# A GLA recurrence on one Trainium2 core: where the output projection's weight sums are held and how many transfers they take, and when the operands of its later products are split

## The chip, the cores and the metric

The kernel runs on one core of a Trainium2 chip. The metric is the time of one execution in device microseconds (us), the median of three executions of the same program. The engines are named as in the profile: PE (TensorE matmul), PEld (its weight loads), DVE (VectorE), ACT (ScalarE), POOL (GpSimd) and SP, whose queue issues the DMA transfers of this kernel.

## The reference

A trunk of two layers over 1024 tokens of width 1024, in float32. Each layer is a token mixer followed by a SwiGLU feed-forward block, both behind an RMS norm and modulated by a conditioning vector `c`. Layer 0 mixes with softmax attention with a forget gate, layer 1 with gated linear attention (GLA). The change lies in layer 1's mixer:

```python
def gated_linear_attention(h, w_in, w_a2, b_a, g_o, w_out):
    q, k, v, r, a_lr = jnp.split(h @ w_in, [512, 1024, 2048, 3072], axis=-1)
    log_alpha = jax.nn.log_sigmoid(a_lr @ w_a2 + b_a) / 16.0
    # 4 heads, 16 chunks of 64 tokens; key width 128, value width 256
    b = jnp.cumsum(log_alpha, axis=2)
    q_in, k_in = q * jnp.exp(b), k * jnp.exp(-b)
    A = jnp.where(tril, jnp.einsum('bnthk,bnshk->bnhts', q_in, k_in), 0.0)
    o_intra = jnp.einsum('bnhts,bnshv->bnthv', A, v)
    kv = jnp.einsum('bnshk,bnshv->bnhkv', k * jnp.exp(b_last[:, :, None] - b), v)
    def step(state, xs):                       # state: (heads, 128, 256)
        dec, kv_n = xs
        return dec[..., None] * state + kv_n, state
    _, s_prev = lax.scan(step, state0, (jnp.exp(b_last), kv))
    o = o_intra + jnp.einsum('bnthk,nbhkv->bnthv', q_in, s_prev)
    o = o * lax.rsqrt(jnp.mean(o * o, axis=-1, keepdims=True) + EPS)   # per head
    return (o.reshape(B, S, 1024) * g_o * jax.nn.silu(r)) @ w_out
```

`x = x + g1 * gla(h)` then goes into the last feed-forward block, and a final RMS norm ends the trunk.

## The kernel before

**Number format.** Every float32 operand of a matmul is held as two parts, hi (a rounding of the value, made by an ACT cast) and lo (the rest, made by a subtraction on DVE or POOL). A product is three matmuls, hi by lo, lo by hi and hi by hi (lines 305, 306 and 307 of the helper `mm3`). `split` (lines 174 and 175) makes the two parts, so each split is one ACT and one DVE instruction. Engines execute their instructions in program order: whatever waits holds up all that stands behind it on its engine or in its queue.

**Stages.** Layer 0 is done by about 1250 us. Then comes layer 1's norm, its first value and gate projections, and from about 1300 to 1640 us the recurrence, one head after the other:

- `head_front` projects keys and queries (tiles `gk_b`, `gqp_b`), scales them with the gate's exponentials and splits them (`gq..`).
- `head_back` computes, in two groups `g` of 512 tokens, the chunks' inner products (`at_b`, masked into `atz_s`, split into `ahl_s`), the outputs `go_b` from the values `gvt_s` and from the state, the state `Sf` (L2115) and its split `S_t`. Each pair of chunks is normalised into `on_t` (L2163; POOL's power for it is L2161), transposed (`ogt_b`, L2125) and multiplied into the gated tile `gs_s` (L2128). The projection of the gate `r` (`gr_b`) is woven between these steps by a planner's costs.
- At a head's end its two `gs_s` tiles (128x1024) go to DRAM (`og_d`, L2280) for heads 0 to 2; those of head 3 stay.
- `gate_body` then makes the next head's exponentials on ACT, and `gv_body` projects its values (`gv_b`, split into `gvt_s`) from two weight tiles `wv_0` and `wv_4`.

**Weights.** Every projection weight is loaded into a ring `wr` of three slots (L227) and split from there by ACT and POOL, the last quarter by DVE (L246). A load into a slot waits until that slot's last reader is done, and so do all transfers behind it in the SP queue. The `ada` work (`ad_s`, loads L442, sums on DVE L505) computes modulation vectors for later stages in the gaps; its loads stand in the same SP queue, its sums in the same DVE program.

**Output projection.** `o @ w_out` is done on blocks of 2x2 with seven products in place of eight, in four column groups `g`. It needs sums of blocks of `w_out`: `ow_sums(h)`, called once a head from `head_front`, loads the four blocks of group `h` into two ring slots (`pw_s`, L971), runs four POOL instructions (L974 to L980) and stores four sums (`ow`, L983). `ow` (L990, L1004, L1005) loads and splits them again later. On the side of `o` the sums are made in `early_t` (heads 0 and 1, woven into head 3) and `out_blocks` (the rest). The products, in the order of the weight index: B11 (`ow` tiles 0 to 3), T2 (4 to 7) and T3 (8 to 11) accumulate in the PSUM banks `oc`; T1 (12 to 15) and B22 (16 to 19) in `oe`; B21 and T4 follow in `out_ends`. `out_add` (L2302) adds a finished bank into the tiles `x`: `x_0`, `x_2`, `x_4` and `x_6` are added first from the B11 product, then from T2. The T3 product of group 0 goes on in the bank that T2's `x_0` addition reads, and so on for the other groups.

**Order.** A scheduler orders the instructions of each engine by priority and due times. `behind_all` makes instructions stand behind those that the table `split_after` names, which before is the last T3 split (L2326). `ob_split(name, j, ...)` makes the split operand of product `name` for the block `j` (tiles `goB` and `goT`).

## Time and profile before

| | |
|---|---|
| median of three executions | 2371.12 us (2369.95 to 2371.66) |
| profiled execution, its own time | 2371.09 us |
| its span, first to last instruction | 2369.4 us |
| granted TensorE clock, mean | 0.998 |
| busy: PE, PEld, DVE, ACT, POOL | 2343.2, 1993.9, 1787.3, 1121.9, 1104.7 us |
| data moved | 375.00 MB, 158 GB/s over the span |

The profile is of one execution: 1.7 us of its time lie outside the span. A row of a timeline reads: start, duration, engine, line, operation, output<-inputs, tile size, count, and in brackets the idle time before it with what ended it. A tile's name has lost its number there. Rows of waits read: engine, line and tile that waited, what it waited for, then total us, times, longest us. "SPq" is SP's queue: a row with it says what a DMA's issue waited for.

### The profile page before, as it was taken

To read this page: it belongs to the slowest core of one execution; us is meant where nothing else is said; L and a number is where in the kernel's file an instruction comes from. 1 tells how busy PE (TensorE), PEld (TensorE's weight loads), DVE (VectorE), ACT (ScalarE), POOL (GpSimd) and SP (SyncE) were. 2 spreads that over 40 slices of the span, in tenths; PEclk is the share of its full clock that TensorE was granted. 3 is DMA by queue.
4 is the path that set the end of the run, shared out by engine and by line. 5 is a ranking of instruction groups with operands and counts; after the bars stand their busy time and mean duration, and the time that the engine had idled before them with its cause. 6 is when DMAs were issued, how large, how long until landed. Compare 5 with 4: busy or idle time off the path is not lost.

```text
span 2369.4 us, 35786 instructions
## 1 busy us (share of the span) xinstructions
PE 2343.2 (99%) x12208; PEld 1993.9 (84%) x12208; DVE 1787.3 (75%) x2994; ACT 1121.9 (47%) x2186; POOL 1104.7 (47%) x995
## 2 busy tenths in 40 slices
PE   8999999999999999999999999999999999999999
PEld 7888888888888888888888899887888888888888
DVE  6577787886688888876788665668787777875787
ACT  6556566665443333345325644344444333345326
POOL 1334444533445665653363432245356665643262
PEclk9999999999999999999999999999999999999999
DMA  8423333332435555457665453454434544457664
GB/s 259 148 77 114 105 121 94 121 126 98 142 103 168 187 165 168 163 195 256 227 210 165 132 148 110 118 185 161 138 106 163 178 147 151 147 200 257 226 201 150
DMA packets 349998, 375.00 MB, mean 158 GB/s; under 512 B 25756, under 2 KB 287032, under 8 KB 349816
## 3 DMA queue, kind: packets, MB, share of 16 engines
q1 hardware_dynamic: 349816, 372.72, 47.9%
q8 instruction: 96, 1.57, 0.3%
q14 instruction: 86, 0.70, 0.1%
HBM read 275.56 MB, written 97.06 MB: 157 GB/s over the span
## 4 chain that ended last, share of the span: by engine, by line
PE 83%; DVE 7%; DMA 3%; issue 2%; POOL 2%; ACT 2%; SPq 1%; DVEq 0%; POOLq 0%; ACTq 0%
PE p_b L305 15%; PE p_b L307 15%; PE p_b L306 15%; PE o_b L1305 2%; PE t_b L1291 2%; PE qk_b L305 2%; PE qk_b L306 2%; PE qk_b L307 2%; PE vps_b L307 1%; PE vps_b L305 1%; PE vps_b L306 1%; PE s_b L1259 1%; PE s_b L1260 1%; PE gr_b L305 1%; PE gr_b L306 1%
## 5 line engine op out<-in xcount | busy, mean ns | idle before, releaser
L175 DVE TENSOR_TENSOR o_s<-xv_s,o_s 128x512 fp32r<-128x512 f32 (+1 forms) x376 | 322.9, 863 | 57.3 <-ACT o_s L174 57.0
L174 ACT CAST o_s<-xv_s 128x512 fp32r<-128x512 f32 (+1 forms) x376 | 216.6, 587 | 297.3 <-PE p_b L307 249.3
L307 PE MATMUL p_b<-B,o_s 128*128 128x512 f32 x608 | 236.0, 389 | 0.0
L306 PE MATMUL p_b<-B,o_s 128*128 128x512 f32 x608 | 235.9, 389 | 0.0
L305 PE MATMUL p_b<-B,o_s 128*128 128x512 f32 x608 | 235.4, 390 | 0.0
L918 POOL TENSOR_TENSOR ex_s<-xv_s,xv_s 128x512 f32<-128x512 f32 (+1 forms) x64 | 90.8, 1419 | 284.2 <-DMA xv_s<-in_ffn_w_in_dram 118.0
L1271 POOL TENSOR_SCALAR lp_s<-lp_s,st 128x128 f32<-128x128 f32 (+7 forms) x128 | 98.0, 769 | 246.6 <-DVE st L1270 230.4
L305 PE MATMUL p_b<-T,o_s 128*128 128x512 f32 x480 | 186.9, 389 | 0.0
L306 PE MATMUL p_b<-T,o_s 128*128 128x512 f32 x480 | 186.8, 389 | 0.0
L307 PE MATMUL p_b<-T,o_s 128*128 128x512 f32 x480 | 181.2, 389 | 0.0
L307 PEld LDWEIGHTS p_b<-B,o_s 128*128 128x128 f32 x608 | 114.1, 188 | 23.9
L305 PEld LDWEIGHTS p_b<-B,o_s 128*128 128x128 f32 x608 | 114.1, 188 | 23.7 <-DVE x L1636 0.2
L306 PEld LDWEIGHTS p_b<-B,o_s 128*128 128x128 f32 x608 | 114.1, 188 | 23.5
L1269 ACT ACTIVATE lp_s<-lp_s,st 128x128 f32<-128x128 f32 (+7 forms) x128 | 99.4, 777 | 58.5 <-DVE st L1265 57.2
L246 POOL TENSOR_TENSOR w_l_s<-w__s,w_h_s 128x256 fp32r<-128x256 f32 x90 | 71.7, 824 | 100.1 <-ACT w_h_s L242 69.2
L920 POOL TENSOR_TENSOR xv_s<-ex_s,xv_s 128x512 f32<-128x512 f32 (+1 forms) x64 | 87.1, 1362 | 63.3 <-DVE o_s L175 61.1
L174 ACT CAST pt_s<-t_b 128x512 fp32r<-128x512 f32 (+1 forms) x160 | 79.7, 547 | 72.6 <-PE t_b L1291 72.0
L1636 DVE TENSOR_TENSOR ex_s<-ex_s,p_b 128x512 f32<-128x512 f32 x140 | 93.6, 680 | 20.7 <-PE p_b L307 20.6
L175 DVE TENSOR_TENSOR pt_s<-t_b,pt_s 128x512 fp32r<-128x512 f32 (+1 forms) x160 | 96.2, 630 | 15.9 <-ACT pt_s L174 15.4
L307 PEld LDWEIGHTS p_b<-T,o_s 128*128 128x128 f32 x480 | 90.1, 188 | 18.7
L306 PEld LDWEIGHTS p_b<-T,o_s 128*128 128x128 f32 x480 | 90.1, 188 | 18.6
L305 PEld LDWEIGHTS p_b<-T,o_s 128*128 128x128 f32 x480 | 90.1, 188 | 18.6
(1803 smaller groups left out, 7438.0 us busy)
## 6 DMA issues: line engine op xcount, KB each, us to landing
xv_s<-in_ffn_w_in_dram SPq DMA_DIRECT2D x176, 256.0 KB, 3.2
hid_B<-x SPq DMA_DIRECT2D x70, 512.0 KB, 3.0
ad_s<-in_ada_w_dram SPq DMA_DIRECT2D x384, 64.0 KB, 2.3
hid_T<-x SPq DMA_DIRECT2D x36, 512.0 KB, 2.9
xv_s<-in_ffn_w_out_dram SPq DMA_DIRECT2D x96, 192.0 KB, 4.8
ada_s<-in_ada_w_dram SPq DMA_DIRECT2D x96, 128.0 KB, 2.8
xv_s<-in_ffn_w_out_dram SPq DMA_DIRECT2D x40, 256.0 KB, 2.9
T2o<-hid_T SPq DMA_DIRECT2D x18, 512.0 KB, 8.3
```

The lines of the kernel that those rows point to most:

```text
L174: nc.scalar.copy(hi, src)
L175: nc.vector.tensor_sub(lo, src, hi.bitcast(F32))
L246: (nc.gpsimd if i < 3 else nc.vector).tensor_sub(lo[:, cs], rw[:, cs], hi[:, cs].bitcast(F32))
L305: nc.tensor.matmul(ps, ah, bh, start=start, stop=False, skip_group_check=chain)
L306: nc.tensor.matmul(ps, ah, bl, start=False, stop=False, skip_group_check=chain)
L307: nc.tensor.matmul(ps, al, bh, start=False, stop=stop, skip_group_check=chain)
L918: nc.gpsimd.tensor_add(s1, a21, a22)
L920: nc.gpsimd.tensor_sub(a11, s1, a11)
L1269: nc.scalar.activation(lp, lp, AF.Exp, bias=mcur, scale=-1.0, accum_out=st[:, qi, 2:3])
L1271: nc.gpsimd.tensor_scalar(lp, lp, st[:, qi, 3:4], 1.0, op0=ALU.mult, op1=ALU.mult)
L1291: nc.tensor.transpose(tp[:, i, :], lps[qi][:, psl(2 * b + jj)], ident)
L1636: nc.vector.tensor_add(d, d if src is None else dest(G, src), ps)
```

## The change

1. `ow_sums` takes its two raw tiles from a ring that it is given, in place of `wr`. For head 0 these are two of the query ring's slots, after the ring is rotated by two, for heads 1 to 3 the two `gs_s` slots that the head before has just filled and stored. Each raw tile is loaded in one transfer of 128x8x128 (512 KB) and stored in one of 128x1024: two loads and two stores a head in place of four and four, 16 in all in place of 32.
2. The sums are begun before the head that they were begun in: for head 0 behind `gate_body(0)`, for the others in the `gv_body` calls at the end of the head before. What is left is run behind `head_front`.
3. In `out_blocks`, for blocks 2 and 3, T3 is formed first (POOL), T2 from it (DVE), and T1 from T2 (DVE) later, behind the point of `behind_all`. Two subtractions go from POOL to DVE.
4. That point is now the last instruction that normalises `on_t` in the last head, in place of the last T3 split.

```diff
--- before.py
+++ after.py
@@ -963,12 +963,12 @@
         src = gla_w_out[0][psl(4 * ab[1], 4), psl(2 * g + ab[0])]
         return src.rearrange("(k p) m -> p k m", p=P)
 
-    def ow_sums(g):
-
-        raw = [wr([P, 2, 4, P], F32, f"pw{g}") for _ in range(2)]
+    def ow_sums(g, ring):
+
+        raw = [ring([P, 2, 4, P], F32, f"pw{g}") for _ in range(2)]
         for i in range(2):
-            for j in range(2):
-                nc.sync.dma_start(raw[i][:, j], ow_src(g, (i, j)))
+            nc.sync.dma_start(raw[i].rearrange("p j k m -> p (j k) m"),
+                              gla_w_out[0][:, psl(2 * g + i)].rearrange("(k p) m -> p k m", p=P))
         (a11, a12), (a21, a22) = ((r[:, 0], r[:, 1]) for r in raw)
         yield
         nc.gpsimd.tensor_add(a22, a21, a22)
@@ -978,9 +978,10 @@
         nc.gpsimd.tensor_sub(a11, a22, a11)
         yield
         nc.gpsimd.tensor_sub(a12, a12, a11)
-        for nm_, r in ((5, a22), (7, a21), (6, a11), (3, a12)):
-            d = ow_d[(nm_, g)] = tc.dram_tile([P, 4, P], F32, name=f"ow{nm_}{g}")
+        for nms, r in (((7, 5), raw[1]), ((6, 3), raw[0])):
+            d = tc.dram_tile([P, 2, 4, P], F32, name=f"ow{g}{nms[0]}")
             nc.sync.dma_start(d, r)
+            ow_d.update({(nm_, g): d[:, j] for j, nm_ in enumerate(nms)})
 
     OW = [(nm_, g) for nm_ in (1, 6, 7, 5, 3, 2, 4) for g in range(4)]
 
@@ -1994,12 +1995,13 @@
         v = vt[-1]
         split(v[:, 0, t % 2], v[:, 1, t % 2], ps[:, 0:256])
 
-    def gv_body(h, wv, tp):
+    def gv_body(h, wv, tp, sums):
 
         ps = pj([P, 2, 256], F32, f"gv{h}{tp}")
         for i in range(2):
             run(proj_tok(ps[:, i, :], wv, h1, 2 * tp + i))
         ada1(5.1)
+        next(sums, None)
         v = vr([P, 2, 2, 256], FR, f"gvt{h}{tp}")
         split(v[:, 0], v[:, 1], ps)
         return v
@@ -2043,12 +2045,10 @@
             nc.scalar.activation(t2[:, psl(n)], b16[:, psl(n)], AF.Exp, scale=1.0 / 16, bias=last[:, n:n + 1])
         return b16, t2, ei, (dec, nmid)
 
-    def head_front(h, b16, t2, ei, nmid):
+    def head_front(h, b16, t2, ei, nmid, sums):
 
 
         wk = feed.next()
-        sums = ow_sums(h)
-        next(sums)
         kin = Pair(kir([P, S], FR, f"kih{h}"), kir([P, S], FR, f"kil{h}"))
         for hf in range(2):
             cs = hsl(hf)
@@ -2056,7 +2056,7 @@
             with ExitStack() if h else tc.issue_after(z_last):
                 run(proj(ps, wk, h1, hf))
             ada1(5.1)
-            next(sums)
+            next(sums, None)
             y = yv()
             nc.vector.tensor_mul(y, ps, ei[:, cs])
             nc.vector.tensor_mul(t2[:, cs], ps, t2[:, cs])
@@ -2077,6 +2077,8 @@
                 nc.vector.scalar_tensor_tensor(y, ps, QS, f[:, cs], op0=ALU.mult, op1=ALU.mult)
                 split(t.hi[:, cs], t.lo[:, cs], y)
         return kin, qt
+
+    on_last = {}
 
     def head_back(h, kin, qt, t2, dec, vt, gs, need):
 
@@ -2161,6 +2163,7 @@
                 nc.gpsimd.tensor_tensor(sst, sst, mhalf[:, 0:2], op=ALU.pow)
                 for i2 in range(2):
                     nc.vector.tensor_scalar(on_t[:, half, i2], o[:, i2, :], sst[:, i2:i2 + 1], None, op0=ALU.mult)
+                on_last.update((e, last_of(e)) for e in "AD")
                 yield 0.01
             yield from og_out(g)
 
@@ -2216,6 +2219,9 @@
     z_last = last_of("P")
     with tc.issue_after(last_of("A")):
         b16, t2, ei, dec = gate_body(0, bt)
+    qr.q.rotate(-2)
+    sums = ow_sums(0, qr)
+    next(sums)
     gtile = {}
     sl_vr, (sl_a, sl_w), sl_t, sl_gs = order[0:5], order[5:7], order[7:10], order[10:12]
     sl_q, sl_ki, sl_kd, sl_y, sl_az, sl_ah, sl_s, sl_on = (order[12:16], order[16:18], order[18:20], *order[20:25])
@@ -2264,7 +2270,8 @@
 
     for h in range(4):
         dec, nmid = dec
-        kin, qt = head_front(h, b16, t2, ei, nmid)
+        kin, qt = head_front(h, b16, t2, ei, nmid, sums)
+        run(sums)
         if h:
             gs = [gsr([P, S], F32, f"gs{h}{i}") for i in range(2)]
             done = set()
@@ -2281,7 +2288,8 @@
         if h < 3:
             b16, t2, ei, dec = gate_body(h + 1)
             wv = [feed.next(), feed.next()]
-            vt = [gv_body(h + 1, wv, tp) for tp in range(4)]
+            sums = ow_sums(h + 1, gsr)
+            vt = [gv_body(h + 1, wv, tp, sums) for tp in range(4)]
 
 
     ada1.flush()
@@ -2317,19 +2325,22 @@
             load_x1(k)
         for j in (2, 3):
             a, c_ = og_t[j], og_t[4 + j]
-            nc.gpsimd.tensor_sub(a[:, h1_], a[:, h0_], a[:, h1_])
-            ob_split("T1", j, a[:, h1_])
-            nc.vector.tensor_sub(a[:, h1_], c_[:, h0_], a[:, h1_])
+            nc.gpsimd.tensor_sub(a[:, h0_], c_[:, h0_], a[:, h0_])
+            nc.vector.tensor_add(a[:, h1_], a[:, h0_], a[:, h1_])
             ob_split("T2", j, a[:, h1_])
-            nc.gpsimd.tensor_sub(a[:, h0_], c_[:, h0_], a[:, h0_])
             ob_split("T3", j, a[:, h0_])
-        split_after.update((e, last_of(e)) for e in "AD")
+        split_after.update(on_last)
         split_after.pop("G", None)
         for j in (0, 1):
             a = og_t[j]
             nc.gpsimd.tensor_sub(a[:, h1_], a[:, h0_], a[:, h1_])
             with behind_all():
                 ob_split("T1", j, a[:, h1_])
+        for j in (2, 3):
+            a = og_t[j]
+            with behind_all():
+                nc.vector.tensor_sub(a[:, h0_], og_t[4 + j][:, h0_], a[:, h1_])
+                ob_split("T1", j, a[:, h0_])
         pa = [bank(g, [P, HALF], f"oc{g}") for g in ALL]
         for g in ALL:
             out_prod(pa[g], feed.next(), ob["B11"], (2, 3, 0, 1), True)
```

In the listings below a name is as in the profile, with its number.

**SP's queue around head 0's sums.** `w__s` and `wv_` are projection weights, `pw_s` the raw blocks, `ow` the stored sums. Before:

```order
L971 DMA pw_s_84_13355<-in_gla_w_out_dram 128x4x128 x2
L442 DMA ad_s_12918<-in_ada_w_dram 32x2x256 x4
L442 DMA ad_s_12919<-in_ada_w_dram 32x2x256 x4
L227 DMA wv_0_s_85_13448<-in_gla_w_in_dram 128x4x256
L983 DMA ow_13538<-pw_s_84_13355 128x512
L983 DMA ow_13540<-pw_s_84_13355 128x512
L983 DMA ow_13542<-pw_s_83_13354 128x512
L983 DMA ow_13544<-pw_s_83_13354 128x512
L442 DMA ad_s_12918<-in_ada_w_dram 32x2x256 x4
L442 DMA ad_s_12919<-in_ada_w_dram 32x2x256 x4
L442 DMA ad_s_12918<-in_ada_w_dram 32x2x256 x4
L227 DMA wv_4_s_86_13561<-in_gla_w_in_dram 128x4x256
```

and with the change:

```order
L970 DMA pw_s_2_13345<-in_gla_w_out_dram 128x8x128
L227 DMA w__s_82_13348<-in_gla_w_in_dram 128x8x128
L970 DMA pw_s_1_13344<-in_gla_w_out_dram 128x8x128
L983 DMA ow_13536<-pw_s_2_13345 128x1024
L983 DMA ow_13538<-pw_s_1_13344 128x1024
L227 DMA wv_0_s_83_13446<-in_gla_w_in_dram 128x4x256
L442 DMA ad_s_12918<-in_ada_w_dram 32x2x256 x4
L442 DMA ad_s_12919<-in_ada_w_dram 32x2x256 x4
L442 DMA ad_s_12918<-in_ada_w_dram 32x2x256 x4
L227 DMA wv_4_s_84_13555<-in_gla_w_in_dram 128x4x256
```

The load of the values' second weight tile, `wv_4`, stood behind the four stores and three batches of `ad_s`; now the raw loads and both stores stand ahead of `wv_0`, and only three batches lie between `wv_0` and `wv_4`.

**SP's queue where head 0's outputs are stored.** `og_d` is the store of a `gs_s` tile; the raw blocks of head 1 go into the same tiles. With the change:

```order
L2287 DMA og_d<-gs_s_1_13095 128x1024
L442 DMA ad_s_12919<-in_ada_w_dram 32x2x256
L442 DMA ad_s_12918<-in_ada_w_dram 32x2x256 x3
L2287 DMA og_d<-gs_s_2_13096 128x1024
L970 DMA pw_s_3_13952<-in_gla_w_out_dram 128x8x128
L442 DMA ad_s_12918<-in_ada_w_dram 32x2x256
L442 DMA ad_s_12919<-in_ada_w_dram 32x2x256 x2
L970 DMA pw_s_4_13953<-in_gla_w_out_dram 128x8x128
L442 DMA ad_s_12919<-in_ada_w_dram 32x2x256 x2
L227 DMA wv_4_s_90_14446<-in_gla_w_in_dram 128x4x256
L442 DMA ad_s_12918<-in_ada_w_dram 32x2x256 x4
```

Before, none of the raw loads stood here:

```order
L442 DMA ad_s_12919<-in_ada_w_dram 32x2x256 x2
L2280 DMA og_d<-gs_s_1_13095 128x1024
L442 DMA ad_s_12919<-in_ada_w_dram 32x2x256 x2
L442 DMA ad_s_12918<-in_ada_w_dram 32x2x256 x3
L2280 DMA og_d<-gs_s_2_13096 128x1024
L442 DMA ad_s_12918<-in_ada_w_dram 32x2x256
L442 DMA ad_s_12919<-in_ada_w_dram 32x2x256 x4
L227 DMA wv_0_s_93_14364<-in_gla_w_in_dram 128x4x256
```

**DVE in the last head, first place.** `Sf` and `S_t` are the state and its split, `goT` and `goB` operand splits, `x_0` to `x_6` the output additions. Before:

```order
L175 TENSOR_TENSOR goT_16477<-og_s_16430,goT_16477 128x512
L175 TENSOR_TENSOR goT_16481<-og_s_16432,goT_16481 128x512
L2302 SCALAR_TENSOR_TENSOR x_2_16450<-oc_16489,modc,x_2_16450 128x512
L175 TENSOR_TENSOR goT_16485<-og_s_16434,goT_16485 128x512
L175 TENSOR_TENSOR goB_16651<-og_s_16649,goB_16651 128x512
L175 TENSOR_TENSOR goB_16654<-og_s_16649,goB_16654 128x512
L175 TENSOR_TENSOR S_t<-Sf_16365,S_t 128x256
L2302 SCALAR_TENSOR_TENSOR x_4_16452<-oc_16490,modc,x_4_16452 128x512
L1005 TENSOR_TENSOR ow_s_8_16565<-wa_s_16078,ow_s_8_16565 128x512
L2302 SCALAR_TENSOR_TENSOR x_6_16454<-oc_16491,modc,x_6_16454 128x512
```

and with the change:

```order
L2165 TENSOR_SCALAR on_t<-go_b_15_16292,gss_16293 128x256 x2
L2329 TENSOR_TENSOR og_s_16406<-og_s_16406 128x512
L2117 SCALAR_TENSOR_TENSOR Sf_16341<-Sf_16311,dec_15603,kv_b_28_16337 128x256
L175 TENSOR_TENSOR goT_16445<-og_s_16406,goT_16445 128x512
L175 TENSOR_TENSOR goT_16442<-og_s_16406,goT_16442 128x512
L2310 SCALAR_TENSOR_TENSOR x_2_16426<-oc_16465,modc,x_2_16426 128x512
L175 TENSOR_TENSOR S_t<-Sf_16341,S_t 128x256
L1006 TENSOR_TENSOR ow_s_8_16541<-wa_s_16054,ow_s_8_16541 128x512
L2310 SCALAR_TENSOR_TENSOR x_4_16428<-oc_16466,modc,x_4_16428 128x512
L2310 SCALAR_TENSOR_TENSOR x_6_16430<-oc_16467,modc,x_6_16430 128x512
```

In these rows the state's last split `S_t` stood behind three `goT` and two `goB` splits and `x_2`; now two `goT` splits, `x_2`, an L2329 and `Sf` itself stand ahead of it.

**DVE in the last head, second place**, the normalisation of the last pair of chunks and T2's addition to `x_0`. Before:

```order
L2160 TENSOR_SCALAR gss_16379<-gss_16379 128x2
L175 TENSOR_TENSOR goB_16730<-gs_s_7_16064,goB_16730 128x512
L2163 TENSOR_SCALAR on_t<-go_b_16_16378,gss_16379 128x256 x2
L2302 SCALAR_TENSOR_TENSOR x_0_16448<-oc_16488,modc,x_0_16448 128x512
L175 TENSOR_TENSOR goB_16638<-og_s_16636,goB_16638 128x512
```

and with the change:

```order
L2162 TENSOR_SCALAR gss_16355<-gss_16355 128x2
L2165 TENSOR_SCALAR on_t<-go_b_16_16354,gss_16355 128x256 x2
L175 TENSOR_TENSOR goT_16449<-og_s_16408,goT_16449 128x512
L175 TENSOR_TENSOR goT_16453<-og_s_16410,goT_16453 128x512
L2342 TENSOR_TENSOR og_s_16404<-gs_s_13_16040,og_s_16404 128x512
L2342 TENSOR_TENSOR og_s_16406<-gs_s_14_16041,og_s_16406 128x512
L175 TENSOR_TENSOR goB_16627<-og_s_16625,goB_16627 128x512
L175 TENSOR_TENSOR goB_16630<-og_s_16625,goB_16630 128x512
L175 TENSOR_TENSOR goB_16706<-gs_s_13_16040,goB_16706 128x512
L175 TENSOR_TENSOR goT_16457<-og_s_16404,goT_16457 128x512
L175 TENSOR_TENSOR goT_16461<-og_s_16406,goT_16461 128x512
L2310 SCALAR_TENSOR_TENSOR x_0_16424<-oc_16464,modc,x_0_16424 128x512
```

The addition to `x_0` followed `on_t` at once; now nine instructions stand between, two of them L2342, the new place of T1's subtractions.

## The prediction, made before the change was run

> **What bounds the kernel now.** I read the engines' busy times first, then the core's clock, then the engines in windows cut at the stages that the change touches, then PE's waits there, and last the timelines around each wait.
>
> ```profile
> PE 2343.2 (99%) x12208; PEld 1993.9 (84%) x12208; DVE 1787.3 (75%) x2994; ACT 1121.9 (47%) x2186; POOL 1104.7 (47%) x995
> core 0: 2369.4 us, clock 0.998
> ```
>
> PE is busy for 2343.2 of 2369.4 us at full granted clock. The change takes no matmul away, so it can win only PE's idle time, 26 us in all, and only that of the stage it touches.
>
> ```profile
> 1321.00:1364.00 43.00, 41.48 (x207) 34.52 (x206) 29.67 (x51) 26.58 (x58) 20.09 (x22) 1.00 0.53 154
> 1364.00:1405.00 41.00, 40.60 (x311) 38.62 (x310) 29.76 (x61) 21.08 (x55) 13.40 (x15) 1.00 0.47 143
> 1405.00:1486.00 81.00, 80.03 (x496) 71.55 (x495) 47.04 (x89) 36.36 (x85) 22.65 (x26) 1.00 0.42 126
> 1486.00:1519.00 33.00, 31.91 (x153) 26.04 (x153) 22.46 (x40) 11.57 (x25) 8.22 (x9) 1.00 0.48 132
> 1519.00:1569.00 50.00, 49.25 (x350) 46.02 (x349) 29.87 (x61) 24.46 (x61) 15.57 (x17) 1.00 0.43 137
> ...
> 1622.00:1652.00 30.00, 26.71 (x128) 21.26 (x127) 29.40 (x37) 14.45 (x31) 21.55 (x17) 1.00 0.46 159
> ```
>
> Columns: window, its length, busy time of PE, PEld, DVE, ACT and POOL, granted clock, DMA share, GB/s. Length less PE's busy time gives the idle time of each: 1.52, 0.40, 0.97, 1.09, 0.75 and 3.29, together 8.02 us. That is all that can be won. In the first five DVE has slack; in 1622 to 1652 it is busy for 29.40 of 30 us and sets the pace. PE's waits name the causes:
>
> ```profile
> PE go_b L306 <- DVE S_t L175: 2.8, 2, 2.4
> PE go_b L305 <- ACT ahl_s L174: 1.9, 2, 1.5
> PE gk_b L305 <- DVE gvt_s L175: 1.0, 1, 1.0
> PE ogt_b L2125 <- DVE on_t L2163: 0.8, 1, 0.8
> PE go_b L305 <- ACT junk L2159: 0.7, 1, 0.7
> PE gr_b L305 <- DVE t_s L2062: 0.5, 1, 0.5
> ```
>
> **Head 0, 1.52 us.** PE waits for `ahl_s`. Ahead of that on ACT stands a weight cast that had waited for its load, and the load had stood in SP's queue behind the sums' stores:
>
> ```profile
> 1338.99 3.01 SPq L983 DMA_DIRECT2D ow<-pw_s  x4
> 1352.32 1.92 SPq L227 DMA_DIRECT2D wv_s<-in_gla_w_in_dram  x1
> 1358.05 1.15 ACT L242 CAST wv_4h_s<-wv_s 128x512 fp32r<-128x512 f32 x2 [4.06 <-DMA wv_s<-in_gla_w_in_dram]
> ```
>
> The changed queue has the raw loads among the keys' and queries' weights and both stores ahead of `wv_0`, and the raw tiles no longer hold weight slots. `wv_4` can then go as soon as its slot is free, several microseconds ahead of 1352.32, and ACT's 4.06 us wait goes with it. I count all 1.52; if three `ad_s` batches still hold `wv_4` back, the least is 0.
>
> **Head 0, second half, 0.31 us, and head 2, 0.97 us.** One of the 0.40 us is PE waiting 0.31 for `S_t`, behind POOL's power, which stood behind a sum (L976, 1379.29, 1.29 us). The sums now leave POOL there: 0.31 won. The 0.97 us is this:
>
> ```profile
> 1379.29 1.29 POOL L976 TENSOR_TENSOR pw_s<-pw_s,pw_s 128x512 f32<-128x512 f32 x1
> SPq L227 <- DMA ow<-pw_s: 5.4, 3, 4.5
> 1477.29 2.88 SPq L442 DMA_DIRECT2D ad_s<-in_ada_w_dram  x4
> 1483.03 0.87 DVE L505 SCALAR_TENSOR_TENSOR ad_s<-ad_s,c 128x256 f32<-128x256 f32 x1 [5.73 <-DMA ad_s<-in_ada_w_dram]
> 1483.82 0.68 DVE L175 TENSOR_TENSOR gvt_s<-gv_b,gvt_s 128x512 fp32r<-128x512 f32 x1
> 1484.56 0.50 PE L305 MATMUL gk_b<-h1h,w_h_s 128*128 128x512 f32 x1 [0.97 <-DVE gvt_s L175]
> 1484.89 0.39 PE L306 MATMUL gk_b<-h1l,w_h_s 128*128 128x512 f32 x1
> 1485.12 0.39 PE L307 MATMUL gk_b<-h1h,w_l_s 128*128 128x512 f32 x1
> ```
>
> A weight load waited up to 4.5 us for a store of the sums to land, the `ad_s` loads stood behind it, and DVE stood 5.73 us at L505 with the values' split next in line. Without that wait the `ad_s` loads go up to 4.5 us earlier, far more than the 0.97 that PE lost. Won: 0.97, least 0 (the loads get a new wait, third rival). The rows also show that the first matmul after a stop starts its successor after 0.33 us in place of 0.23: each stop costs about 0.1 more. Five stops that go give 0.5.
>
> **Head 2's front, 1.09 us.** Here DVE's quarter of a weight split waits for a cast whose weights came late, again by the slots that the sums held:
>
> ```profile
> 1502.67 0.55 DVE L246 TENSOR_TENSOR w_l_s<-w__s,w_h_s 128x256 fp32r<-128x256 f32 x1 [2.40 <-ACT w_h_s L242]
> 1515.53 0.66 PE L2089 MATMUL kdt_b<-ident,t_s 128*128 128x128 f32 x4 [0.21 <-DVE kdl_s L175]
> 1517.43 0.39 PE L305 MATMUL go_b<-gvt_s,ahl_s 128*128 128x256 f32 x1 [0.42 <-ACT ahl_s L174]
> ```
>
> DVE gets 2.40 us back and PE's three waits are 0.5, 0.21 and 0.42. I take 0.8, since the exponentials and splits between are not changed; bounds 0 and 1.09.
>
> **Head 3's start, 0.75 us** (PE behind ACT's `junk`): the exponentials ahead of it stay, and an `S_t` cast may now stand behind them too. I take 0, bounds +0.7 and -0.7.
>
> **The output stage, 3.29 us.** The largest piece:
>
> ```profile
> 1623.31 1.13 DVE L175 TENSOR_TENSOR goT<-og_s,goT 128x512 fp32r<-128x512 f32 x1
> 1623.84 1.74 POOL L2320 TENSOR_TENSOR og_s<-og_s 128x512 f32<-128x512 f32 x1
> 1624.36 1.51 DVE L175 TENSOR_TENSOR S_t<-Sf,S_t 128x256 fp32r<-128x256 f32 x1
> 1632.03 1.27 DVE L2322 TENSOR_TENSOR og_s<-gs_s,og_s 128x512 f32<-128x512 f32 x1
> 1633.22 0.68 DVE L175 TENSOR_TENSOR goT<-og_s,goT 128x512 fp32r<-128x512 f32 x1
> 1642.45 1.48 DVE L175 TENSOR_TENSOR S_t<-Sf,S_t 128x256 fp32r<-128x256 f32 x1
> 1643.98 0.39 PE L306 MATMUL go_b<-S_t,gq31h_s 128*128 128x256 f32 x1 [2.44 <-DVE S_t L175]
> 1648.14 0.88 DVE L2163 TENSOR_SCALAR on_t<-go_b,gss 128x256 f32<-128x256 f32 x2 [0.59 <-POOL gss L2161]
> 1648.94 0.74 DVE L2302 SCALAR_TENSOR_TENSOR x<-oc,modc,x 128x512 f32<-128x512 f32 x1
> 1652.07 0.39 PE L305 MATMUL oc<-goT,ow_s 128*128 128x512 f32 x1
> ```
>
> The state's last split (1642.45) stands behind product splits on a full DVE, and PE waits 2.44 us for it, and 0.8 us for `on_t`. The change brings that split forward past three `goT`/`goB` splits, worth 2.0 to 3.4 us at 0.68 to 1.13 each, so those waits shrink or vanish. But DVE's work is not less. Ahead of T2's addition to `x_0` (1648.94) it now has the same thirteen operand splits from this `Sf` on and two subtractions more. T3's matmuls (1652.07) go on in the bank that this addition reads, so PE cannot pass it. The price: two L2342, at 1.27 us (the nearest row, a subtraction of the same form) 2.54 us, less the 0.59 us wait ahead of `on_t`, which the earlier `S_t` removes: the addition starts at 1648.94 + 2.54 - 0.59 = 1650.89, ends 0.74 later, at 1651.6, and T3 starts then. PE without stops would be there at 1652.07 - 3.29 = 1648.8. So the stage wins 1652.07 - 1651.6, about 0.5 us; a new wait of some 2.9 us takes the place of the 3.29. Bounds: with the two at 0.68 (nothing on POOL) and none of the other operations slowed, 1.7; with 1.78, the longest of L2322 in the stage, and both L2329 standing for the POOL subtraction that now precedes them (1.3 each, by L976), 1648.94 + 3.56 + 2.6 - 0.59 + 0.74 = 1655.25, a loss of 3.2.
>
> The longest L2322:
>
> ```profile
> 1628.93 1.78 DVE L2322 TENSOR_TENSOR og_s<-gs_s,og_s 128x512 f32<-128x512 f32 x1
> ```
>
> DVE's operations stretch at some places: the 128x256 split at 1624.36 took 1.51 us beside POOL's L2320, where twice as many elements took 0.68 at 1633.22.
>
> **Edits that cost nothing.** Half as many raw transfers are eight loads and eight stores fewer, each some 0.75 us of SP's time (four took 3.01 above); PE waits for none of them directly. POOL's sums keep their sixteen instructions of 1.29 us, at other places, where POOL has over half its time free (the first five windows). If head 0's first sum waits for its load, POOL stands a microsecond ahead of a memset that is not due.
>
> **Sum.** 1.52 + 0.31 + 0.97 + 0.8 + 0 + 0.5 + 0.5 = 4.6 us, against the profiled execution's 2371.09 (2369.4 of span, 1.7 around it, 0.03 from the median): **2366.5 us**.
>
> **The rivals.** *First, POOL's lighter load frees DVE.* POOL loses two L2320 (the one above 1.74 us), which ran beside stretched DVE operations. If DVE regains 0.5 to 1 us at each and the subtractions run beside an idle POOL, T2's addition ends near 1649 and T3 has no wait: another 2.7 us, **2363.8**. For it: 1.51 against 0.68. Against it: the rest of POOL's sums and weight splits go on there (21.55 us busy of 30), and L2329 now waits for POOL.
>
> [...]
>
> *Second, DVE stays the bound and the front wins half.* `S_t` moves, T3 waits half a microsecond longer than in the forecast so that the stage wins nothing, and of the 3.6 us upstream half goes: 2371.1 - 1.8 = **2369.3**. For it: DVE's 29.40 of 30 us. Against it: the waits upstream are each traced to a transfer that moves.
>
> *Third, slower: the raw loads wait in SP's queue for the outputs' stores.* For heads 1 to 3 they go into the tiles that `og_d` has just sent, and these loads stand right behind the stores:
>
> ```profile
> og_d<-gs_s SPq DMA_DIRECT2D x6, 512.0 KB, 3.0
> ```
>
> Each store lands 3.0 us after its issue, so the queue stands up to 3 us for each of the two tiles, with `ad_s` loads behind, and DVE at L505 with the values' splits behind that, as at 1483.03. There the cover is used up (PE stops already), so each further microsecond is one of PE's: 6 at most a head change, 3.5 as a middle, 10.5 us for three: 2366.5 + 10.5 = **2377**. It decides from (2375.9 - 2366.5) / 3 = 3.1 us a head change. Against it: the two stores are issued some microseconds apart, so the first has landed when its load comes up, and four `ad_s` loads take 2.88 us to issue (1477.29), so little stands in the way of the queue.
>
> *Fourth, the change does nothing where it counts*: PE's stops in the front come from the order of DVE's program, not from the queue, and stay; 2371 less 0.5.
>
> **How the numbers follow.** Forecast 0.50, its own range 2364.5 to 2368.5; first rival 0.16, second 0.13, third 0.14, fourth 0.07. A measurement of this kernel tells a difference from none at about 0.2%, 4.7 us: faster is below 2366.4, slower above 2375.9. The forecast lies on that edge; of its 0.50 I put 0.26 below it. Faster: 0.26 + 0.16 = 0.42. Within: 0.24 + 0.13 + 0.07 = 0.44. Slower: 0.14. For 8 in 10 the range goes from 2362.5, which all 8.02 us and the restarts would give, to 2373, which takes in the second and fourth rivals and a mild third.
>
> **What would show it.** In the changed profile PE's waits for `ahl_s` (1.5) and `gvt_s` (1.0) should be gone, and ACT's 4.06 us wait for `wv_s`. PE's 2.44 us wait for `S_t` should be below 1, with a new wait of 2 to 3 us of `oc` (T3) for DVE's L2310, the new number of L2302's line. If `oc` has no wait, the first rival holds; if SP's queue shows L970 waiting for `og_d` for over 2 us a head and PE waits behind L505, the third. The prediction is wrong if PE's idle time between 1300 and 1652 falls by less than 2 or more than 7 us.

## The result and the profile after

| | before | changed |
|---|---|---|
| median of 14 executions | 2370.58 us | 2363.47 us |
| lowest to highest | 2365.85 to 2374.92 | 2362.06 to 2367.89 |
| span of the profiled execution | 2369.4 us | 2361.5 us |
| granted TensorE clock | 0.998 | 0.998 |

The ratio of the times is 0.9972 (95% interval 0.9964 to 0.998): 0.28% faster, 7.1 us between the medians. In a second comparison, with 11 executions, it was 0.9979 (0.997 to 0.9988), 5.3 us. The forecast was 2366.5 us in a range of 2362.5 to 2373, with 0.42 on faster and 0.44 on no difference; by its own mark, below 2366.4, the change is faster.

The first thing to read is PE's waits of the changed kernel from 1250 to 1720 us (what waited, for what, total us, times, longest):

```profile
PE gv_b L307 <- POOL h1l L745: 0.8, 1, 0.8
PE oc L305 <- DVE x L2310: 0.5, 1, 0.5
PE rb_b L727 <- POOL rs L715: 0.5, 1, 0.5
PE at_b L306 <- DVE gq10l_s L175: 0.4, 1, 0.4
PE kdt_b L2091 <- DVE kdl_s L175: 0.2, 1, 0.2
```

None of the six waits shown of before is left. New are 0.8 us for a split of the norm (`h1l`), 0.5 us of T3 for T2's addition (`oc`, L2310), 0.5 us in the next stage's norm, and 0.4 us for a query split (`at_b`). To say where the time came from I cut both traces at one place, the DVE weight subtraction that follows the last head's third `on_t` from the end (`ow_s`, L1005 before, L1006 now), and read PE's busy time from 1300 us to it and for 52 us from it on. Of before, and of the changed kernel:

```profile
1300.00:1617.12 317.12, 312.39 (x1904) 277.47 (x1904) 200.15 (x368) 153.22 (x358) 107.45 (x115) 1.00 0.46 140
1617.12:1669.12 52.00, 48.71 (x234) 39.66 (x233) 48.33 (x61) 24.57 (x52) 36.68 (x27) 1.00 0.44 144
```
```profile
1300.00:1612.28 312.28, 310.85 (x1903) 277.39 (x1902) 201.30 (x367) 152.95 (x358) 105.06 (x115) 1.00 0.47 142
1612.28:1664.28 52.00, 51.51 (x248) 42.45 (x247) 47.96 (x65) 26.27 (x55) 34.85 (x26) 1.00 0.45 150
```

Below, the first stretch is called the front, the second the output stage. PE's idle time fell from 4.73 to 1.43 us in the front and from 3.29 to 0.49 us in the output stage. The cut itself comes 4.84 us earlier (1612.28 against 1617.12), although layer 1's norm starts at the same time in both traces (its first `rb_b` matmul at 1279.29 and 1279.27), and T3's first matmul comes 8.12 us earlier:

```profile
1643.07 0.73 DVE L2310 SCALAR_TENSOR_TENSOR x<-oc,modc,x 128x512 f32<-128x512 f32 x1
1643.95 0.47 PE L305 MATMUL oc<-goT,ow_s 128*128 128x512 f32 x1 [0.49 <-DVE x L2310]
1714.18 1.04 PE L727 MATMUL rb_b<-ident,rs 128*128 128x128 f32 x7 [0.46 <-POOL rs L715]
```

Before, T3 started at 1652.07. So in these two executions 4.8 us came from the front and 3.3 us from the output stage. The span ends 7.8 us earlier, 0.3 less than T3: at 1714 PE now waits 0.46 us for the next norm's row sums. The other traces, below, make both parts smaller on average.

### The profile page after: what moved, and what is told of

Its sections match the earlier page's. It is cut to its first block, busy times and chain, and to the rows that moved or that the text cites. A ratio compares the mean times of both kernels' runs of the same rounds, so it can differ in the third digit from the quotient of the medians.

```text
span 2361.5 us, 35758 instructions
## 1 busy us (share of the span) xinstructions
PE 2340.8 (99%) x12208; PEld 1994.0 (84%) x12208; DVE 1786.5 (76%) x2996; ACT 1122.4 (48%) x2186; POOL 1102.5 (47%) x993
```

## The experiments

"Front" and "output" are PE's idle us in the two stretches; the cut is the same instruction in each kernel. "Norm to cut" is the time from the first `rb_b` matmul of layer 1's norm to the cut. "To x_0" is the time on DVE from the cut to T2's addition to `x_0`. "Clock" is the mean granted clock of the output stage. The time is the median of 5 to 14 executions, and the ratio's interval is against before in the same comparison (before's medians: 2369.56 for e1 to e4, 2369.26 for e6 to e9, 2368.8 for the rest). For e9 and e10 the time is that of one execution.

| kernel | us | ratio to before | front | norm to cut | output | clock | to x_0 |
|---|---|---|---|---|---|---|---|
| before | 2370.58 | | 4.73 | 337.83 | 3.29 | 1.00 | 31.82 |
| changed | 2363.47 | 0.9964 to 0.998 | 1.43 | 333.01 | 0.49 | 1.00 | 30.79 |
| changed, again | 2363.54 | 0.997 to 0.9988 | 0.81 | 332.49 | 1.61 | 1.00 | 31.89 |
| e1 sums only | 2367.69 | 0.9981 to 0.9999 | 3.70 | 335.70 | 2.60 | 1.00 | 29.80 |
| e2 output only | 2364.62 | 0.9971 to 0.9988 | 3.35 | 336.00 | 1.87 | 1.00 | 31.40 |
| e3 point back | 2367.15 | 0.998 to 0.9998 | 1.07 | 332.79 | 2.80 | 0.97 | 30.56 |
| e4 T1 on POOL | 2367.93 | 0.9982 to 0.9999 | 1.88 | 333.62 | 2.85 | 0.97 | 30.39 |
| e6 32 transfers | 2370.43 | 0.9996 to 1.0014 | 4.60 | 339.07 | 2.86 | 1.00 | 33.99 |
| e7 16 transfers only | 2369.48 | 0.9991 to 1.001 | 3.19 | 336.10 | 3.34 | 0.97 | 31.78 |
| e8 old ring | 2372.41 | 1.0005 to 1.0024 | 8.30 | 340.93 | 1.86 | 1.00 | 31.38 |
| e9 POOL reads | 2370.25 | | 1.86 | 333.53 | 6.03 | 0.97 | 36.27 |
| e10 POOL writes | 2366.59 | | 1.48 | 333.42 | 2.21 | 0.97 | 32.22 |
| f1 | 2360.65 | 0.9955 to 0.998 | 1.31 | 332.85 | 1.58 | 1.00 | 31.86 |
| f3 | 2362.17 | 0.9961 to 0.9982 | 0.47 | 331.89 | 0.00 | 1.00 | 27.27 |

A caution on single rows: up to the cut, every engine of before and of e2 runs the same instructions in the same order, and the two show 4.73 and 3.35 us of idle time. The changed kernel, its repeat, e1, e3, e4, e9 and e10 also share one program there, and show 0.81 to 3.70. From the norm to the cut the first two take 337.83 and 336.00 us, the other seven 332.49 to 335.70: means of 336.9 and 333.5, so the front's part is 3.4 us on average where the pair above shows 4.8. And ahead of the norm, where no two of these kernels differ, the first `rb_b` matmul starts between 1275.1 us (e3) and 1280.7 (f3). One execution settles a mechanism by the row that shows it, not a microsecond of its time.

### Which part wins where: e1, e2, e3

e1 has the sums of the changed kernel with the old `out_blocks`, e2 the sums of before with the new `out_blocks` and its `on_last`. e3 is the changed kernel with one line:

```diff
-        split_after.update(on_last)
+        split_after.update((e, last_of(e)) for e in "AD")
```

> Only the weight sums' part of the change (buffers, transfers, earlier start); the order of T1, T2 and T3 and the point of behind_all are those of before. Theory (two independent gains: about 4.1 us from the front by the sums, about 3.1 us from the output stage by the order there): PE's waits for ahl_s (1.5) and gvt_s (1.0) are gone, the 2.4 us wait for S_t in the last head stays, time 4 us below before, about 2366.5 against 2370.6. Rival (the sums' early place also frees DVE and POOL in the last head, and the output stage's gain comes from there): nearly all of the gain, 6 to 7 us below before.

> Only the output stage's part (T3 first, T1 later, the point of behind_all at the last on_t); the sums are those of before. Theory: the front's waits (ahl_s 1.5, gvt_s 1.0, junk 0.7) stay, the wait for S_t in the last head goes, T3 waits 0.5 us or less for the addition to x_0, time 3 us below before, about 2367.5 against 2370.6. Rival (as in the forecast, T3 waits some 2.9 us for x_0 when the sums do not help): 0 to 0.5 us below before.

> The changed kernel with the point of behind_all put back to the last T3 split. Theory (the point brings the last S_t forward): S_t stands behind two L2342 and some five splits more, PE waits 2 to 3 us for it again, time 2 to 3 us above the changed kernel, 2365.5 to 2366.5. Rival (forming T3 first and two POOL subtractions less are enough): the same time as the changed kernel within 0.7 us.

e1's median is 1.9 us below before's and e2's 4.9 us, together 6.8, about what the whole change gives (7.1 and 5.3 in its two comparisons). That fits two separate gains, each uncertain by some 2 us by its interval, and e1's rival, nearly all of the gain, fell. But e6 and e8, below, have the new `out_blocks` too and are no faster than before, so the parts don't simply add. e1 won 1.9 us where its theory said 4. Its profiled execution is the slowest of its eleven (2370.95 us), and PE's waits in it show one cause; the first row is in head 1:

```profile
PE at_b L305 <- ACT gq10h_s L174: 2.2, 1, 2.2
PE oc L305 <- DVE x L2307: 1.4, 2, 1.0
PE ogt_b L2125 <- DVE on_t L2163: 1.2, 2, 1.0
```

The waits for `ahl_s` and `gvt_s` are gone, but a stop of 2.2 us has come for a query split. The changed kernel has the same instructions there and waits 0.4 us, its repeat 0.6. The sums' new place left a wait of uncertain length, DVE's L505 for its `ada` blocks (3.23 us in the changed kernel, 4.16 in e1), with the query splits behind it. Also, the 2.4 us wait for `S_t` did not stay as expected; it is 0, with waits of 1.4 and 1.2 us for other DVE work in its place, and T3 starts 33.06 us behind the cut, 34.95 in before. So part of the output stage's gain came in e1 too, with the old `out_blocks`; why is not shown. In e2, which won 4.9 us where its theory said 3, two of the three expected waits of the front stay:

```profile
PE oc L305 <- DVE x L2305: 1.9, 2, 1.6
PE go_b L305 <- ACT ahl_s L174: 1.5, 2, 1.1
PE go_b L305 <- ACT junk L2161: 0.8, 1, 0.8
```

The third, for `gvt_s` (0.97 us in before), is absent from e2 with the same program, so it differs between executions of one program. In e2 T3 waits 1.6 us, not the 0.5 of the theory nor the rival's 2.9. e3 shows the expected wait, and a time 2.4 us below before, where 4 to 5 were expected: with the point put back the state's last split is late again, PE's only long wait is the first row below, and the clock falls behind it (second row, from 1634 to 1637.5: granted clock 0.55).

```profile
PE go_b L306 <- DVE S_t L175: 2.7, 1, 2.7
```
```profile
1634.00:1637.50 3.50, 3.50 (x11) 2.80 (x11) 3.50 (x5) 1.53 (x5) 0.80 (x1) 0.55 0.28 82
```

So it is the point of `behind_all` that brings `S_t` forward. In the kernels with the old point (before, e1, e3, e7) DVE starts the last `S_t` 24.3 to 25.3 us behind the cut, in the changed kernel, its repeat, e2 and e8, with the new one, 16.6 to 18.9.

### Buffers and transfers: e6, e7, e8

e6 is the changed kernel with two loads and two stores for each raw tile (`for j in range(2): nc.sync.dma_start(raw[i][:, j], ow_src(g, (i, j)))`, and likewise the stores); e7 is before with only the halved transfers; e8 is the changed kernel with `ow_sums(0, wr)` and `ow_sums(h + 1, wr)`.

> The changed kernel with 32 transfers of 256 KB for the sums' raw blocks and results in place of 16 of 512 KB; buffers, start and output stage as changed. Theory (the buffers and the start carry the front's gain, the number of transfers does not): no wait of PE for ahl_s or gvt_s, the front within 1 us of the changed kernel. Rival (the number of transfers in SP's queue counts): SP's queue is 16 issues longer, about 12 us by 0.75 us each, weights and ada blocks come later and 2 us or more of the front's 4 us are lost again.

> The kernel before with 16 transfers of 512 KB in place of 32 of 256 KB for the sums; buffers, start and output stage as before. Theory: within 1 us of before, the waits for ahl_s and gvt_s stay. Rival: 2 us or more below before.

> The changed kernel with the sums' raw tiles in the weight ring of three slots again; 16 transfers, earlier start and output stage as changed. Theory (the weight loads were late because the raw tiles held their slots): SP's queue waits for the stores to land again, PE waits again in the front for splits that stand behind weights or ada blocks, 2 to 5 us above the changed kernel. Rival (the earlier start alone is enough): within 1 us of the changed kernel.

The halved transfers alone win nothing (e7), as expected. Without them the new buffers and the earlier start win nothing either (e6), which refutes the theory: e6 lost all of the gain. In head 2 DVE and PE wait like this:

```profile
1505.27 0.48 DVE L505 SCALAR_TENSOR_TENSOR ad_s<-ad_s,c 128x256 f32<-128x256 f32 x1 [6.28 <-DMA ad_s<-in_ada_w_dram]
1509.77 0.67 DVE L2062 TENSOR_TENSOR t_s<-gk_b,t_s 128x512 f32<-128x512 f32 x1
```
```profile
PE gr_b L305 <- DVE t_s L2062: 2.8, 1, 2.8
```

The changed kernel's DVE stops at the same place for nearly as long, and PE does not wait:

```profile
1502.57 1.00 DVE L505 SCALAR_TENSOR_TENSOR ad_s<-ad_s,c 128x256 f32<-128x256 f32 x2 [5.46 <-DMA ad_s<-in_ada_w_dram]
1505.57 0.68 DVE L2062 TENSOR_TENSOR t_s<-gk_b,t_s 128x512 f32<-128x512 f32 x1
```

So in e6 `t_s` starts 4.2 us later. Of that, 2.7 us are the `ada` blocks, which come later: four stores in place of two stand in SP's queue behind POOL's sums and ahead of them. The other 1.5 us are DVE's order, which has more work between L505 and `t_s`: the scheduler places DVE's and SP's instructions in heads 1 to 3 in another order when the transfers change. The end of this chain, DVE at L505 with PE behind it, is that of the prediction's third rival, but no raw load waits for an output's store here. Its loss in the output stage (2.86 us), where DVE's order is another too, is not traced further. e8 shows what the buffers are for. With the weight ring back, the raw loads wait for their slots as they did in before (34.5 us, there 32.9; the changed kernel's longest such wait is 6.0), SP's queue waits for the stores again, five times and for 9.5 us in all, and the front's idle time is 8.30 us:

```profile
SPq L970 <- DVE w_l_s L246: 34.5, 3, 17.9
```
```profile
SPq L227 <- DMA ow<-pw_s: 9.5, 5, 3.5
```

Its time is 3.2 us above before's and some 9 above the changed kernel's, where 2 to 5 were expected. In these kernels both had to be there, slots that no weight load waits for and the shorter queue; as each kernel also has its own order, the share of each is not shown.

### What stretches DVE: e4, e9, e10

In e4 the late L2342 is `nc.gpsimd.tensor_sub`. In e9 and e10 six weight subtractions on POOL get additional work in front, which leaves the result as it is (in e9 the first of the two lines below, in e10 the second):

```diff
+        if n % 4 in OW_G and 3 < n < 12:
+            nc.gpsimd.tensor_sub(t[:, 1], r, t[:, 0].bitcast(F32))      # e9
+            for _ in range(2): nc.gpsimd.memset(t[:, 1].bitcast(F32), 0.0)   # e10
```

> The changed kernel with T1's two late subtractions on POOL in place of DVE. Theory (DVE's two-input operations stretch while POOL works): DVE has two operations of 1.15 us less ahead of the addition to x_0, but its splits go back from 0.74 to about 0.9 to 1.1 us each, so x_0 comes less than 1 us earlier and the time is within 0.7 us of the changed kernel. Rival (only the number of DVE's own operations counts): x_0 comes 2.3 us earlier, T3's wait of 0.49 is gone, 0.6 us below the changed kernel, and the splits keep their 0.74.

> The changed kernel with the lo part of six projection weights subtracted twice on POOL (the same result twice) in the output stage: 6 more POOL operations of 1.3 us that read two tiles. Theory (a POOL operation that reads blocks a DVE operation with two tile inputs): the DVE splits that run beside them take 1.1 to 1.8 us in place of 0.68, T2's addition to x_0 comes 1 to 4 us later after the last head's on_t(14), and T3 waits longer than 0.49 us for it. Rival (DVE is slowed by its own load or the DMA, not by POOL): the shares of slow and quick splits stay, x_0 and T3 within 0.5 us.

> The changed kernel with two more POOL writes of constants (128x512, about 0.5 us each) ahead of each of six weight subtractions in the output stage; they read nothing. Theory (only POOL operations that read block two-input DVE operations): DVE splits of 128x512 beside these writes take 0.68 us, T3 waits for x_0 about as in the changed kernel, below 1.5 us. Rival (any POOL operation blocks): splits beside them take 1.0 us or more and T3 waits over 2 us.

The clearest pair is one instruction, the addition that forms T2 (L2329, in e10 L2332), which starts as POOL goes on to the next work. In the changed kernel POOL's next work is a weight subtraction, in e10 four writes of zeros:

```profile
1620.48 3.00 POOL L1006 TENSOR_TENSOR ow_s<-xv_s,ow_s 128x512 fp32r<-128x512 f32 x2
1620.56 1.76 DVE L2329 TENSOR_TENSOR og_s<-og_s 128x512 f32<-128x512 f32 x1 [1.41 <-POOL og_s L2328]
```
```profile
1620.42 1.93 POOL L1008 MEMSET ow_s<- 128x512 f32 x4
1620.51 0.69 DVE L2332 TENSOR_TENSOR og_s<-og_s 128x512 f32<-128x512 f32 x1 [1.41 <-POOL og_s L2331]
1621.51 1.28 DVE L175 TENSOR_TENSOR goT<-og_s,goT 128x512 fp32r<-128x512 f32 x2
```

1.76 us beside a POOL instruction that reads, 0.69 beside one that only writes. Over the output stages of before and of the changed kernel, all 19 DVE splits of 128x512 with no POOL instruction beside them took 0.67 to 0.68 us, and the 29 with one took 0.68 to 1.79.

The changed kernel and its repeat show the same without any edit. They run one program; in the first, POOL's L2363 waited 0.68 us for a load and began when the second of the last two `goT` was under way, in the repeat it lay across that split. The two `goT` took 2.37 and 3.47 us, and `x_0` came 30.79 and 31.89 us behind the cut:

```profile
1640.77 2.37 DVE L175 TENSOR_TENSOR goT<-og_s,goT 128x512 fp32r<-128x512 f32 x2
1642.67 1.61 POOL L2363 TENSOR_TENSOR og_s<-og_s,og_s 128x512 f32<-128x512 f32 x1 [0.68 <-DMA og_s<-og_d]
```
```profile
1640.86 3.47 DVE L175 TENSOR_TENSOR goT<-og_s,goT 128x512 fp32r<-128x512 f32 x2
1642.07 1.71 POOL L2363 TENSOR_TENSOR og_s<-og_s,og_s 128x512 f32<-128x512 f32 x1
```

e9's `x_0` came 5.5 us later than the changed kernel's (36.27 against 30.79), 4.4 later than in the repeat. 2.3 us of that is not stretch but queue: DVE waits 3.10 us for POOL's small power, in place of 0.81, as the power stands behind the doubled work, which the theory had not counted. Here are that wait, and T3's for `x_0`:

```profile
1636.88 0.88 DVE L2167 TENSOR_SCALAR on_t<-go_b,gss 128x256 f32<-128x256 f32 x2 [3.10 <-POOL gss L2165]
```
```profile
1647.52 0.76 PE L305 MATMUL oc<-goT,ow_s 128*128 128x512 f32 x1 [4.61 <-DVE x L2312]
```

In e10 T3 waited 2.2 us, as its rival said and not the theory, but by another way than the rival's: beside the writes both L2332 stayed short, at 0.69 and 0.68 us. The last two `goT` took 3.48 us, as in the repeat of the changed kernel (3.47), where T3 waited 1.6, and the wait ahead of `on_t` was 1.25 in place of 0.81. e4 took two instructions off DVE, 2.4 us, and `x_0` came 0.4 us earlier than in the changed kernel and 1.5 earlier than in its repeat, not 2.3. The state's split beside POOL's new subtraction is one of those that pay for it (0.42 us in the changed kernel):

```profile
1625.04 1.68 POOL L2342 TENSOR_TENSOR og_s<-gs_s,og_s 128x512 f32<-128x512 f32 x1 [0.62 <-DVE goT L175]
```
```profile
1625.48 1.51 DVE L175 TENSOR_TENSOR S_t<-Sf,S_t 128x256 fp32r<-128x256 f32 x1
```

e4 was not within 0.7 us of the changed kernel, as its theory said, but only 1.6 us below before, where the changed kernel is 5.3 to 7.1 below: a later addition, behind other stretched splits, held T3 for 2.1 us and the granted clock fell (mean 0.66 from 1653 to 1658 us).

### What was left to win: f1, f3

f1 queues head 0's sums on POOL behind the norm's last `h1l`. f3 also puts T1's late subtractions behind T2's addition to `x_0`:

```diff
+            with ExitStack() if h else tc.issue_after(norm_g):
+                next(sums, None)
...
+            with behind_all(), tc.issue_after(x0_add):
+                nc.vector.tensor_sub(a[:, h0_], og_t[4 + j][:, h0_], a[:, h1_])
+                ob_split("T1", j, a[:, h0_])
```

> The changed kernel with head 0's first sum queued on POOL behind the last h1l of the norm. Theory: PE's 0.8 us wait for h1l goes with its restart, 1.0 us below the changed kernel in the trace between 1300 and 1330. Rival: the sums' stores come later, SP's queue with wv_0 behind them too, and PE waits 0.5 us or more at 1340 to 1390 instead.

> As f1, and T1's two late subtractions and their splits also behind T2's addition to x_0. Theory: x_0 comes some 4 us earlier on DVE (two L2342 of 1.15 us and two splits), T3's wait of 0.49 us goes, 0.65 us more. Rival: T1's operands come too late for the products into oe, and PE waits there for goT, 1 us or more.

> The changed kernel itself, for a comparison on the same chip: 7 us below before; PE waits in the front 0.8 for h1l and 0 to 2.5 for at_b, and 0.5 for x_0.

Both waits went in f3 as expected: `x_0` came 27.27 us behind the cut, T3 did not wait, and T1's operands were not late. PE's waits of f3 between 1300 and 1740 us are:

```profile
PE at_b L306 <- DVE gq10l_s L175: 0.2, 1, 0.2
PE kdt_b L2092 <- DVE kdl_s L175: 0.2, 1, 0.2
```

Its two stretches have 0.47 us idle where the changed kernel had 1.92 and, in its repeat, 2.42. The medians (2360.65 for f1, 2362.17 for f3, 2363.54 for the changed kernel in the same comparison) lie in this order, but their intervals overlap: that f3 is faster than the changed kernel is shown by waits, not by time. For f1 it is not shown at all: its two stretches have 2.89 us idle, with 1.6 for `x_0` and 0.7 for `t_s` in head 2; its rival's wait at 1340 to 1390 us did not come. The wait for `h1l` is itself not constant: of the nine other kernels that begin the sums early, seven have it, the changed kernel's repeat and e8 do not.

## Why the prediction was right, and where it was off

**The number.** The time lies in the range, 1.0 us below the forecast's own 2364.5 to 2368.5. The 4.6 us forecast are short of the 7.1 of the first comparison and near the 5.3 of the second. Its output term was too small and its front term, 4.1, above the traces' average of 3.4, so part of the error cancels.

**Head 0 and head 2's front** (1.52, 0.31, 0.8 us): right. These waits are gone in the changed kernel and there in e2 (1.12, 0.31 and 1.15). Gone too is ACT's 4.06 us wait for `wv_4`; its longest wait for a weight load from 1320 to 1365 us is now this:

```profile
ACT wv_0h_s L242 <- DMA wv_s<-in_gla_w_in_dram: 1.7, 1, 1.7
```

That the raw tiles' slots held the loads up is shown by e8, which gives them back; the waits of PE that return there are others, though (for `on_t`, `Sf` and `kdl_s`).

**The splits of the values** (0.97 us): gone, but not by the change as far as is shown. e2 has a DVE stop of 4.91 us at the same L505, and PE does not wait. The changed kernel's DVE stops 5.46 us for `ada` blocks later in head 2, so such a stop is still there, at a place where PE does not wait behind it.

**Half as many transfers at no price:** wrong as a statement on the front. e7 shows that alone they win nothing, e6 that in its order the front's gain does not come without them.

**Head 0's first sum on POOL** was priced at nothing, "a memset that is not due". Behind the memsets stand the norm's last `h1l` splits, and PE waited 0.8 us for one. In f1 and f3 it does not, nor in the repeat.

**Head 3's start** (0.75 us, taken as staying): gone in the changed kernel and in e1, still there in e2. The sums' part removes it.

**The front as a whole:** 3.6 us of waits and 0.5 of restarts were forecast. PE's idle time fell by 3.30 us, and the cut came 4.84 us earlier, or 3.4 on the average of nine traces. Where the time beyond the idle time lies was not traced.

**The output stage** is the term that was mis-sized: 0.5 us forecast, 3.3 measured (2.8 of it idle time), and 2.2 in the repeat, where T3 starts 32.78 us behind the cut (before 34.95, changed 31.67). The mechanism was right. `S_t` came forward, and T3 then waited for T2's addition to `x_0`. What was off is the time of that addition, "1648.94 + 2.54 - 0.59 = 1650.89", 1.95 us later than before. It came 1.03 us earlier relative to the cut, and 0.07 us later in the repeat, so T3 waited 0.49 and 1.6 us for it, not 2.9. (By the same sum the better bound is a gain of 1.6, not 1.7.) DVE's groups between the cut and the addition, before (the columns: count, busy us and mean ns, idle before):

```profile
L175 DVE TENSOR_TENSOR goT<-og_s,goT 128x512 fp32r<-128x512 f32 x9 | 8.5, 962 | 0.0
L175 DVE TENSOR_TENSOR goB<-og_s,goB 128x512 fp32r<-128x512 f32 x6 | 6.8, 1163 | 0.0
L175 DVE TENSOR_TENSOR S_t<-Sf,S_t 128x256 fp32r<-128x256 f32 x3 | 4.5, 1497 | 0.0
...
L2322 DVE TENSOR_TENSOR og_s<-gs_s,og_s 128x512 f32<-128x512 f32 x2 | 3.1, 1527 | 0.0
L2163 DVE TENSOR_SCALAR on_t<-go_b,gss 128x256 f32<-128x256 f32 x5 | 2.2, 475 | 0.6 <-POOL gss L2161 0.6
```

and in the changed kernel:

```profile
L175 DVE TENSOR_TENSOR goT<-og_s,goT 128x512 fp32r<-128x512 f32 x8 | 7.3, 945 | 0.0
L175 DVE TENSOR_TENSOR goB<-og_s,goB 128x512 fp32r<-128x512 f32 x6 | 4.8, 842 | 0.0
...
L2329 DVE TENSOR_TENSOR og_s<-og_s 128x512 f32<-128x512 f32 x2 | 3.5, 1762 | 1.4 <-POOL og_s L2328 1.4
L2342 DVE TENSOR_TENSOR og_s<-gs_s,og_s 128x512 f32<-128x512 f32 x2 | 2.4, 1226 | 0.0
L175 DVE TENSOR_TENSOR S_t<-Sf,S_t 128x256 fp32r<-128x256 f32 x3 | 2.3, 779 | 0.0
L2165 DVE TENSOR_SCALAR on_t<-go_b,gss 128x256 f32<-128x256 f32 x5 | 2.2, 475 | 0.8 <-POOL gss L2163 0.8
```

The two L2342 cost what was forecast (2.4 against 2.54). The wait ahead of `on_t` did not go (0.8 against 0.6), and L2329 did wait for POOL once (1.4), which the forecast had kept for its upper bound, and took 0.4 more than L2322. Against these 4.4 us stand savings that it had not counted: the three `S_t` splits fell by 2.2 us, the `goB` splits by 2.0, one `goT` less stands between the cut and the addition (1.2), and a weight subtraction fell by 0.4. The count of thirteen splits from `Sf` on was right; ahead of `Sf` before had three splits and the changed kernel two. The shorter splits fit the pair of rows above (1.76 us beside a weight subtraction on POOL, 0.69 beside e10's writes): two subtractions fewer on POOL, and more of the splits at places where POOL reads nothing. How much is the fewer subtractions and how much the places is not shown.

**The rivals.** The first, that POOL's lighter load frees DVE (2363.8, chance 0.16), has the right mechanism and lies within 0.4 us of the measured time, but T3 kept a wait, 0.49 us in one trace and 1.6 in the repeat, f1, e2 and e8, where the rival had none. That the time agrees so closely is partly luck. It deserved more: the rows 1.51 us beside POOL and 0.68 elsewhere were on the page, and the sum went by the durations of before as though they belonged to the instruction. The second (the stage wins nothing) and the fourth (the front's waits stay) did not occur, though DVE's stops at L505 stayed, as the fourth had it of DVE's program. The third (slower, the queue) did not occur either: SP's queue shows no wait of L970 for `og_d`.

## What to carry to other kernels

A duration in a profile belongs to an instruction and its neighbour (the same addition took 1.76 us beside a POOL subtraction and 0.69 beside writes): before pricing a move between DVE and POOL by the nearest row, sort that engine's rows by whether the other was reading beside them. Transfers that can be joined may win nothing where they stand (e7, 0.9991 to 1.001 of before) and still go with another move's gain (without them e6 is at 0.9996 to 1.0014); test such parts singly and together. And where a schedule is rebuilt by a planner, "the same kernel with one part undone" is another order as well, so look at its waits before its time.

## What the runs showed of the hardware

In some of these runs a stop of PE cost more than its length. At the end of e9's stop of 4.61 us the granted clock fell to 0.50 for 3.41 us, and matmuls started about 0.43 us apart in place of 0.23:

```profile
1647.15:1650.56 3.41, 3.04 (x7) 2.48 (x8) 3.41 (x5) 1.14 (x2) 3.41 (x3) 0.50 0.09 26
```

e3 (2.7 us), e4 (2.1 us), e7 (2.4 us) and e10 (2.2 us) show the same 3.41 us at 0.50, e6 (2.8 us) twice that; the 2.44 us stop of before and the 2.2 us stop of e1 do not, and no stop of 1.6 us or less in these stretches does. Before and e7 have the same stop for `S_t`, 2.44 us long. In the profile of before the clock stayed full, in that of e7 it fell 1.7 us behind the stop's end (1638.44):

```profile
1644.00:1647.00 3.00, 3.00 (x13) 2.37 (x14) 3.00 (x6) 1.89 (x5) 1.07 (x1) 1.00 0.37 87
```
```profile
1640.12:1643.53 3.41, 3.41 (x9) 2.62 (x8) 2.82 (x7) 2.49 (x7) 2.04 (x2) 0.50 0.66 220
```

So stops of 2.1 to 2.8 us were followed by the lower clock in five executions (e3, e4, e6, e7, e10), and stops of 2.44 and 2.2 us in two others (before, e1) were not; what decides between them is not shown. An estimate from the lengths and the clock of 0.50: 3.41 us at half the clock are at most 1.7 us lost, and e6's 6.83 us (1509.34 to 1516.17) at most 3.4. So in part of the executions a wait of two to three microseconds, as before had in its output stage, cost by this estimate nearly that much again, which a sum over one profiled execution does not hold.
